# An encoder layer on one core: a longer last and first step at the two block boundaries, operand places on one grid, modulation pieces summed one per step, both transposes of a block in one go

## The chip, the cores and the metric

The kernel runs on one core of a Trainium2 chip. The metric is device time in microseconds of one launch. What is compared is the median of several executions; the profile is one execution, recorded in full.

## The reference

One layer of a bidirectional encoder over 256 positions of width 2048, float32, batch 1. Nine modulation vectors (a shift, a scale and a gate for each of three blocks) come from one product of silu(c) with a 2048 x 18432 matrix.

```python
mod = silu(c) @ w_ada + b_ada                   # sh1, sc1, g1, sh2, sc2, g2, sh3, sc3, g3
h = rms_norm(x, ffn1_pre_g) * (1 + sc1) + sh1   # modulate
x = x + 0.5 * g1 * rms_norm((silu(h @ w_gate) * (h @ w_up)) @ w_down, ffn1_post_g)
h = rms_norm(x, mix_pre_g) * (1 + sc2) + sh2
q, k, v, c_val, c_gate = split(h @ w_in)        # 8 heads of 128; conv branch of 1024
merged = concat([rms_norm(attention), rms_norm(conv branch)]) @ w_out
x = x + g2 * rms_norm(merged, mix_post_g)
h = rms_norm(x, ffn2_pre_g) * (1 + sc3) + sh3
x = x + 0.5 * g3 * rms_norm((silu(h @ w_gate) * (h @ w_up)) @ w_down, ffn2_post_g)   # D_FF = 5632
```

## The kernel before

The 256 positions are two halves t of 128 rows. Every weight matrix is read from HBM once, in chunks of 256 rows x 512 columns (512 KB, `wchunk`, L280): a load from SP's queue into one of 7 `raw` buffers, a rounding copy `hi` on ScalarE (L290), and the rest `lo` = raw - hi on VectorE (L291), in 4 buffer pairs. The activations are kept as hi and lo too. For each 128-row slice k of a chunk, and each half t, TensorE makes three products of 512 columns (L316 to L318: hi with xh, lo with xh, hi with xl), the weights moving and the activations stationary; a chunk is 12 products. `in_step` (L320) loads the chunks it is given, then multiplies all of them for t = 0 and after that all for t = 1, and ticks. A tick starts work put off by `defer` and lets each lane (a generator) advance by its rate.

`group` (L329) takes a whole product chunk by chunk; with `tail=4` the last four chunks are one step, so half 0 is done ahead of half 1, and with `head=4` the first four are.

A block boundary is `next_norm` (L409). The last group's half t is evicted (`ffn_down` L459, or L880), squared and summed (`post_block`), the four sums give a factor by way of GpSimd's pow (`post_rstd`), x is updated in four pieces and squared again (`post_add`, L405), a second pow gives the next norm's factor, and `pre_norm` (L360) scales x (`xn`, L368), transposes it on TensorE (L371), applies scale and shift on ScalarE (`hf`, L376) and splits it (L357, L358). There are two such boundaries: FFN1 to the mixer, whose first group `c0` is 8 chunks of w_in, and the mixer to FFN2, whose `begin2` takes the first gate and up group of stage 0 (two chunks each) as one step.

The modulation vectors are not products of TensorE: `mod_sum` (L169) loads 512 KB pieces of w_ada through the same `raw` buffers and adds them on VectorE, `acc = piece * c + acc` (L191), for a scale and a shift in turn; TensorE and ScalarE then sum over partitions (L206, L211). This runs as a lane beside the products. FFN1 is entered in four stages of K (`STAGES1`), FFN2 in three (`STAGES2`), so that products start while later slices of the modulation are still being summed; pieces are 512 columns wide (two sums a piece) or, for the last third of a FFN2 stage, 256 wide (four sums a piece).

`slot` (L249) hands out the shared places of a work pool by tag (`hh0`.., `ah0`.., `fs0`.., `gs`, `ac`). A place is 4096 bytes a partition, the two with tags `ah5` and `al5` are SLOT = 1144 elements, 4576 bytes. The places lie one after the other in order of first use, `al5` right behind `ah5`. `al5` holds the low part of the sixth block of `aT`.

In FFN's up products, `act_out` (L423) puts off the transposes of a finished block by `defer(AD, ..)` and `defer(AD + 1, ..)`: four transposes each, two chunks apart from the block's end and three. `rope_T` does the same for q and k.

## Time and profile before

| | us |
|---|---|
| median of 3 runs (lowest to highest) | 1952.46 (1952.25 to 1954.24) |
| the profiled execution | 1953.91 |
| its span | 1952.1 |
| TensorE busy | 1872.6 |
| VectorE busy | 1474.1 |
| ScalarE busy | 928.3 |

The span runs from the first instruction to the last; the profiled execution's own time is 1.8 us above it and 1.45 us above the median. Busy time of TensorE is an upper bound, since overlapping products count as busy to their modelled ends. Its granted clock is 1.00 (2.4 GHz) or 0.5 (1.2 GHz); a value between is a mean over a stretch.

### The profile page before, as it was taken

To read this page: it belongs to the slowest core of one execution; us is meant where nothing else is said; L and a number is where in the kernel's file an instruction comes from. 1 tells how busy PE (TensorE), PEld (TensorE's weight loads), DVE (VectorE), ACT (ScalarE), POOL (GpSimd) and SP (SyncE) were. 2 spreads that over 40 slices of the span, in tenths; PEclk is the share of its full clock that TensorE was granted. 3 is DMA by queue.
4 is the path that set the end of the run, shared out by engine and by line. 5 is a ranking of instruction groups with operands and counts; after the bars stand their busy time and mean duration, and the time that the engine had idled before them with its cause. 6 is when DMAs were issued, how large, how long until landed. Compare 5 with 4: busy or idle time off the path is not lost.

```text
span 1952.1 us, 23783 instructions
## 1 busy us (share of the span) xinstructions
PE 1872.6 (96%) x8358; PEld 1527.1 (78%) x8358; DVE 1474.1 (76%) x1824; ACT 928.3 (48%) x1428; POOL 66.0 (3%) x99
## 2 busy tenths in 40 slices
PE   2999999999999999899999988999999999999997
PEld 1888877888888888688888776687888888888886
DVE  6789999787777776689997777897786556545455
ACT  3554355444444444644456655534444443444442
POOL 2000000000000000000100000000000000000000
PEclk9999999999999999899999999999999999999999
DMA  9989978999999898357555767897777777666653
GB/s 344 310 297 311 323 253 283 348 340 328 314 321 316 317 318 292 109 184 224 173 165 161 239 214 258 301 341 254 226 247 244 244 253 248 195 185 191 206 191 101
DMA packets 250392, 496.29 MB, mean 254 GB/s; under 512 B 17209, under 2 KB 42625, under 8 KB 250272
## 3 DMA queue, kind: packets, MB, share of 16 engines
q1 hardware_dynamic: 247888, 491.38, 76.1%
q0 software_dynamic: 2208, 3.32, 0.5%
q8 instruction: 65, 1.06, 0.2%
q14 instruction: 55, 0.45, 0.1%
q10 hardware_dynamic: 176, 0.07, 0.0%
HBM read 492.58 MB, written 2.12 MB: 253 GB/s over the span
## 4 chain that ended last, share of the span: by engine, by line
PE 88%; DVE 5%; DMA 3%; ACT 2%; issue 2%; POOL 0%; DVEq 0%; POOLq 0%; ACTq 0%; SPq 0%
PE pd_t L318 8%; PE pd_t L317 8%; PE pd_t L316 8%; PE pg_t L317 8%; PE pg_t L318 8%; PE pg_t L316 8%; PE pu_t L318 8%; PE pu_t L317 8%; PE pu_t L316 7%; PE pc_t L316 2%; PE pc_t L318 2%; PE pc_t L317 2%; DVE acc L191 2%; DMA ada<-in_w_ada 1%; PE pa L384 1%
## 5 line engine op out<-in xcount | busy, mean ns | idle before, releaser
L191 DVE SCALAR_TENSOR_TENSOR acc<-ada,cact,acc 128x512 f32<-128x512 f32 (+2 forms) x448 | 384.9, 897 | 12.8 <-DMA acc<-in_b_ada 8.4
L291 DVE TENSOR_TENSOR lo_d<-raw_d,hi_d 128x1024 fp32r<-128x1024 f32 x176 | 215.3, 1225 | 157.6 <-ACT hi_d L290 156.9
L290 ACT CAST hi_d<-raw_d 128x1024 fp32r<-128x1024 f32 x176 | 185.2, 1052 | 261.2 <-PE pd_t L318 181.5
L290 ACT CAST hi_g<-raw_g 128x1024 fp32r<-128x1024 f32 x176 | 185.0, 1052 | 247.2 <-PE pg_t L318 121.0
L291 DVE TENSOR_TENSOR lo_g<-raw_g,hi_g 128x1024 fp32r<-128x1024 f32 x176 | 214.4, 1222 | 105.0 <-ACT hi_g L290 104.8
L291 DVE TENSOR_TENSOR lo_u<-raw_u,hi_u 128x1024 fp32r<-128x1024 f32 x176 | 213.9, 1222 | 104.7 <-ACT hi_u L290 104.4
L290 ACT CAST hi_u<-raw_u 128x1024 fp32r<-128x1024 f32 x176 | 184.8, 1052 | 214.0 <-PE pu_t L318 94.5
L318 PE MATMUL pd_t<-hi_d,a_0l 128*128 128x512 f32 x384 | 151.2, 394 | 0.0
L317 PE MATMUL pd_t<-lo_d,a_0h 128*128 128x512 f32 x384 | 150.5, 392 | 0.0
L316 PE MATMUL pd_t<-hi_d,a_0h 128*128 128x512 f32 x384 | 150.4, 392 | 0.0
L316 PE MATMUL pg_t<-hi_g,h3h 128*128 128x512 f32 x352 | 140.4, 401 | 5.3 <-ACT hi_g L290 4.2
L316 PE MATMUL pu_t<-hi_u,h3h 128*128 128x512 f32 x352 | 139.8, 400 | 2.9 <-ACT hi_u L290 2.9
L317 PE MATMUL pu_t<-lo_u,h3h 128*128 128x512 f32 x352 | 140.0, 398 | 1.7 <-DVE lo_u L291 1.6
L317 PE MATMUL pg_t<-lo_g,h3h 128*128 128x512 f32 x352 | 139.4, 396 | 1.7 <-DVE lo_g L291 1.7
L316 PE MATMUL pg_t<-hi_g,h1h 128*128 128x512 f32 x352 | 139.4, 398 | 1.0 <-ACT hi_g L290 1.0
L318 PE MATMUL pu_t<-hi_u,h3l 128*128 128x512 f32 x352 | 139.7, 397 | 0.0
L317 PE MATMUL pg_t<-lo_g,h1h 128*128 128x512 f32 x352 | 138.7, 394 | 0.8 <-DVE lo_g L291 0.8
L318 PE MATMUL pg_t<-hi_g,h3l 128*128 128x512 f32 x352 | 139.3, 396 | 0.0
L316 PE MATMUL pu_t<-hi_u,h1h 128*128 128x512 f32 x352 | 138.8, 396 | 0.0
L318 PE MATMUL pu_t<-hi_u,h1l 128*128 128x512 f32 x352 | 138.6, 394 | 0.0
L318 PE MATMUL pg_t<-hi_g,h1l 128*128 128x512 f32 x352 | 138.6, 395 | 0.0
L317 PE MATMUL pu_t<-lo_u,h1h 128*128 128x512 f32 x352 | 137.8, 392 | 0.1
(259 smaller groups left out, 3572.1 us busy)
## 6 DMA issues: line engine op xcount, KB each, us to landing
ada<-in_w_ada SPq DMA_DIRECT2D x288, 512.0 KB, 5.3
raw_g<-in_ffn_w_gate SPq DMA_DIRECT2D x176, 512.0 KB, 4.7
raw_u<-in_ffn_w_up SPq DMA_DIRECT2D x176, 512.0 KB, 4.7
raw_d<-in_ffn_w_down SPq DMA_DIRECT2D x176, 512.0 KB, 5.7
raw_c<-in_w_in SPq DMA_DIRECT2D x64, 256.0 KB, 3.1
raw_q<-in_w_in SPq DMA_DIRECT2D x16, 512.0 KB, 4.4
raw_k<-in_w_in SPq DMA_DIRECT2D x16, 512.0 KB, 4.5
raw_v<-in_w_in SPq DMA_DIRECT2D x16, 512.0 KB, 4.2
```

Source lines behind the costliest of these rows:

```text
L191: tc.keep_in_program_order(nc.vector.scalar_tensor_tensor(acc, w[:, j, :], cact[:, j0 + j:j0 + j + 1], acc, op0=ALU.mult, op1=ALU.add))
L290: nc.scalar.copy(h, r)
L291: nc.vector.tensor_tensor(l, r, f32(h), op=ALU.subtract)
L316: nc.tensor.matmul(o, xh, h, start=self.first and k == 0, stop=False)
L317: nc.tensor.matmul(o, xh, l, start=False, stop=False)
L318: nc.tensor.matmul(o, xl, h, start=False, stop=self.last and k == self.nk - 1)
L384: nc.tensor.transpose(ps[:, jj * S + t * P:jj * S + (t + 1) * P], src[:, t, jj * P:(jj + 1) * P], ident)
```

## The change

`mod_sum` loads and sums one piece and then yields, where it loaded a scale's and a shift's piece and summed both in turn. `group` loses `head`; the last step of FFN's last group is 7 chunks (`TAIL1`), and the last step of the mixer is both of the last two output blocks, 8 chunks. Three and four chunks of these steps get `hi`/`lo` in places of the work pool (`TAIL_AT1`, `TAIL_AT2`). The next block's first chunks are loaded before `next_norm`, four of them into such places (`HEAD_AT1`, `HEAD_AT2`); its first step is all 8 chunks of `c0`, or three groups of FFN2's stage 0 (6 chunks). Eviction of half t moves into `next_norm`. The SLOT size becomes a multiple of 64 elements, and a 64-byte tile `gap` is put ahead of the `h` places. The two deferred transposes of a block become one.

```diff
@@ -35,10 +35,14 @@
-HEAD = 4
-TAIL = 4
 JF = 4
+TAIL1 = 7
+TAIL_AT1 = (("hh2", "hl2"), ("hh3", "hl3"), ("gs", "ac"))
+HEAD1 = 8
+HEAD_AT1 = (("ah0", "al0"), ("ah1", "al1"), ("ah2", "al2"), ("ah3", "al3"))
+HEAD_AT2 = TAIL_AT2 = (("ah0", "ah1"), ("ah2", "ah3"), ("al2", "al3"), ("ah5", "al5"))
 CRATE = 1.8
...
@@ -51,7 +55,7 @@
 RAW = 7
 HILO = 4
-SLOT = 4 * (S + 2 * PAD)
+SLOT = -(-4 * (S + 2 * PAD) // 64) * 64
 STAGES1 = ((0, 4), (4, 8), (8, 12), (12, 16))
 STAGES2 = ((0, 4), (4, 10), (10, 16))
...
@@ -178,20 +182,16 @@
             accs.append(acc)
         kt = CH * BLK // n
         for j0 in range(0, NK, kt):
-            ws = []
-            for v in vs:
+            for v, acc in zip(vs, accs):
                 n0 = v * D + c0
                 raw = wpool.tile([P, CH, BLK], F32, tag="raw", bufs=RAW, name=f"ada{v}_{c0}_{j0}")
                 w = raw.rearrange("p a b -> p (a b)").rearrange("p (j n) -> p j n", n=n)
                 nc.sync.dma_start(w, w_ada[j0 * P:(j0 + kt) * P, n0:n0 + n].rearrange(
                     "(j p) n -> p j n", p=P))
-                ws.append(w)
-            for j in range(kt):
-                for w, acc in zip(ws, accs):
+                for j in range(kt):
                     tc.keep_in_program_order(nc.vector.scalar_tensor_tensor(
                         acc, w[:, j, :], cact[:, j0 + j:j0 + j + 1], acc,
                         op0=ALU.mult, op1=ALU.add))
-            for v in vs:
                 yield
         return accs
...
@@ -277,11 +277,16 @@
             return self.lo[k // 4][:, k % 4:k % 4 + n, :]
-    def wchunk(w, r0, kt, cols, name):
+    def wchunk(w, r0, kt, cols, name, at=None):
         raw = wpool.tile([P, CH, BLK], F32, tag="raw", bufs=RAW, name=f"raw_{name}")
-        hi = wpool.tile([P, CH, BLK], F32R, tag="hi", name=f"hi_{name}")
-        lo = wpool.tile([P, CH, BLK], F32R, tag="lo", name=f"lo_{name}")
+        if at is None:
+            hi = wpool.tile([P, CH, BLK], F32R, tag="hi", name=f"hi_{name}")
+            lo = wpool.tile([P, CH, BLK], F32R, tag="lo", name=f"lo_{name}")
+        else:
+            hi = slot(at[0], [P, CH, BLK], f"hi_{name}", F32R)
+            lo = slot(at[1], [P, CH, BLK], f"lo_{name}", F32R)
         r, h, l = raw[:, :kt, :], hi[:, :kt, :], lo[:, :kt, :]
         n = BLK // len(cols)
         for m, n0 in enumerate(cols):
...
@@ -317,22 +322,26 @@
                 nc.tensor.matmul(o, xh, l, start=False, stop=False)
                 nc.tensor.matmul(o, xl, h, start=False, stop=self.last and k == self.nk - 1)
-    def in_step(work):
-        hls = [g.load(c) for g, c in work]
+    def load_all(work, places=()):
+        return [g.load(c, places[n] if n < len(places) else None) for n, (g, c) in enumerate(work)]
+    def in_step(work, places=(), hls=None):
+        if hls is None:
+            hls = load_all(work, places)
         for t in range(NT):
             for (g, c), hl in zip(work, hls):
                 g.products(c, t, hl)
         for _ in work:
             tick()
-    def group(*args, head=0, tail=0, **kw):
+    def group(*args, tail=0, places=(), **kw):
         g = Group(*args, **kw)
-        head = min(head, g.chunks - tail)
-        mid = range(head, g.chunks - tail)
-        for cs in (range(head), *([c] for c in mid), range(g.chunks - tail, g.chunks)):
-            in_step([(g, c) for c in cs])
+        for c in range(g.chunks - tail):
+            in_step([(g, c)])
+        if tail:
+            in_step([(g, c) for c in range(g.chunks - tail, g.chunks)], places)
     def square_sum(src, dst, name):
...
@@ -406,18 +415,17 @@
             square_sum(xs, sx[:, db:db + 1], "jx")
         return rstd_parts(sx, D, f"r{i}_{t}", keep_in="rx")
-    def next_norm(f, ssp, A, B, j1, i):
-        hT = Parts(f"h{i}", "h", range(4))
-        jh = min(HEAD * CH, j1)
+    def next_norm(hT, f, ssp, A, B, j1, i, evict):
+        evict(0)
         rs = [post_add(f, post_rstd(ssp, i, 0), i, 0)]
         pre_norm(hT, rs, A, B, 0, JF, i, 0, 1)
+        evict(1)
         rs.append(post_add(f, post_rstd(ssp, i, 1), i, 1))
-        pre_norm(hT, rs, A, B, JF, jh, i, 0, 1)
-        pre_norm(hT, rs, A, B, 0, jh, i, 1, 2)
-        pre_norm(hT, rs, A, B, jh, j1, i)
-        return hT, rs
+        pre_norm(hT, rs, A, B, JF, j1, i, 0, 1)
+        pre_norm(hT, rs, A, B, 0, j1, i, 1, 2)
+        return rs
     def act_out(aT, i, gs, pu, name):
...
@@ -430,9 +438,12 @@
             src = transposed(ac[:, :, q * 256:(q + 1) * 256], tr_ps(f"pa{name}_{q}"))
             split_to(aT, k0 + 2 * q, 2, src)
+        def turns():
+            turn(0)
+            turn(1)
         aT.add(i)
-        defer(AD, lambda: turn(0))
-        defer(AD + 1, lambda: turn(1))
+        defer(AD, turns)
     def gs_tile(name):
         return work.tile([P, NT, BLK], F32, tag="gs", name=f"gs{name}")
...
@@ -451,14 +462,19 @@
         for db in range(4):
             pd = mm_ps(f"pd{i}_{th}_{db}")
             group(pd, aT, wd, ba * 4, (bb - ba) * 4, db * BLK, f"d{i}_{th}_{db}",
-                  tail=TAIL if th == 1 and db == 3 else 0)
-            for t in range(NT):
+                  tail=TAIL1 if th == 1 and db == 3 else 0, places=TAIL_AT1)
+            def evict(t, db=db, pd=pd):
                 if th == 0:
                     nc.scalar.copy(f[db][:, t, :], pd[t])
                 else:
                     nc.vector.tensor_tensor(f[db][:, t, :], pd[t], f[db][:, t, :], op=ALU.add)
-                if th == 1:
                     post_block(f, ssp, G, t, db)
+            if th == 1 and db == 3:
+                return evict
+            for t in range(NT):
+                evict(t)
     ROUNDS = ((0, 6, (0, 1, 2, 3, 4, 5)), (6, 11, (0, 1, 2, 3, 5)))
...
@@ -562,17 +578,15 @@
     rs = [rstd_parts(sx[t], D, f"r0_{t}", act=True, keep_in="rx") for t in range(NT)]
     for _ in first:
         pass
+    nc.vector.memset(work.tile([P, 16], F32, name="gap"), 0.0)
     hT = Parts("h1", "h", range(4))
     pre_norm(hT, rs, A1, B1, *STAGES1[0], "1_0")
     def begin2(open_group, run, order):
-        gs, k1 = {}, STAGES2[0][1]
-        for w, b in order[:2]:
-            ps = mm_ps(f"p{w}2_{b}_0")
-            gs[w, b] = open_group(w, b, 0, 0, k1, ps)
-        in_step([(g, c) for g in gs.values() for c in range(g.chunks)])
-        return {k: (g.ps, k1) for k, g in gs.items()}, k1
+        in_step(ahead2, hls=hls2 + load_all(ahead2[4:]))
+        return {k: (g.ps, STAGES2[0][1]) for k, g in heads2.items()}, len(ahead2)
     load_cols(("conv_b", "conv_ln_g", "conv_ln_b", "attn_out_g", "conv_out_g"), 1)
     g1, g2, g3 = [keep.tile([P, NK], F32, name=f"gc{i}") for i in (1, 2, 3)]
...
@@ -586,10 +600,17 @@
     aT = ffn_start(hT, a["ffn1_w_gate"], a["ffn1_w_up"], 1, STAGES1, ffn1_mods,
                    lambda s: pre_norm(hT, rs, A1, B1, *STAGES1[s], f"1_{s}"),
                    (later_mods(), LRATE))
-    f, ssp = ffn_rest(hT, aT, a["ffn1_w_gate"], a["ffn1_w_up"], a["ffn1_w_down"],
-                      lambda: gate_tile(g1, 1), 1)
+    f, ssp, evict = ffn_rest(hT, aT, a["ffn1_w_gate"], a["ffn1_w_up"], a["ffn1_w_down"],
+                             lambda: gate_tile(g1, 1), 1)
     drain_all()
-    hT, rs = next_norm(f, ssp, A2, B2, NK, 2)
+    QC = BLK // 2
+    hT = Parts("h2", "h", range(4))
+    ps_c0 = mm_ps("pc0")
+    c0 = Group(ps_c0, hT, a["w_in"], 0, NK, (3 * AW, 3 * AW + CW), "c0")
+    ahead = [(c0, c) for c in range(HEAD1)]
+    hls = load_all(ahead[:4], HEAD_AT1)
+    rs = next_norm(hT, f, ssp, A2, B2, NK, 2, evict)
+    in_step(ahead, hls=hls + load_all(ahead[4:]))
     w_in = a["w_in"]
...
@@ -654,8 +675,11 @@
             pst = transposed(ra[:, :, q * 256:(q + 1) * 256], tr_ps(f"prt_{name}_{q}"))
             nc.scalar.copy(T[:, 2 * q:2 * q + 2, :], pst)
-        defer(RD, lambda: turn(0))
-        defer(RD + 1, lambda: turn(1))
+        def turns():
+            turn(0)
+            turn(1)
+        defer(RD, turns)
         return T
     scale = HD ** -0.5
...
@@ -873,22 +896,46 @@
     drain(conv_entry)
     drain(mods)
     r2 = rc["conv"]
-    for db in range(4):
-        po = mm_ps(f"pc{db}")
-        group(po, mT, w_out, 8, 8, db * BLK, f"oc{db}", kx=8, tail=TAIL if db == 3 else 0)
-        for t in range(NT):
-            nc.vector.scalar_tensor_tensor(f[db][:, t, :], po[t], r2[:, t:t + 1],
-                                           f[db][:, t, :], op0=ALU.mult, op1=ALU.add)
-            post_block(f, ssp, G2, t, db)
-    hT, rs = next_norm(f, ssp, A3, B3, STAGES2[0][1], 3)
+    pcs = [None] * 4
+    def conv_group(db):
+        pcs[db] = mm_ps(f"pc{db}")
+        return Group(pcs[db], mT, w_out, 8, 8, db * BLK, f"oc{db}", kx=8)
+    def evict_c(db, t):
+        nc.vector.scalar_tensor_tensor(f[db][:, t, :], pcs[db][t], r2[:, t:t + 1],
+                                       f[db][:, t, :], op0=ALU.mult, op1=ALU.add)
+        post_block(f, ssp, G2, t, db)
+    for db in range(2):
+        g = conv_group(db)
+        for c in range(g.chunks):
+            in_step([(g, c)])
+        for t in range(NT):
+            evict_c(db, t)
+    both = [conv_group(db) for db in (2, 3)]
+    in_step([(g, c) for g in both for c in range(g.chunks)], TAIL_AT2)
+    def evict(t):
+        for db in (2, 3):
+            evict_c(db, t)
+    hT = Parts("h3", "h", range(4))
+    heads2 = {}
+    for w, b in (("g", 0), ("u", 0), ("g", 1)):
+        heads2[w, b] = Group(mm_ps(f"p{w}2_{b}_0"), hT, a["ffn2_w_gate" if w == "g" else "ffn2_w_up"], 0,
+                             STAGES2[0][1], b * BLK, f"{w}2_{b}_0_0")
+    ahead2 = [(g, c) for g in heads2.values() for c in range(g.chunks)]
+    hls2 = load_all(ahead2[:4], HEAD_AT2)
+    rs = next_norm(hT, f, ssp, A3, B3, STAGES2[0][1], 3, evict)
     aT = ffn_start(hT, a["ffn2_w_gate"], a["ffn2_w_up"], 2, STAGES2, ffn2_mods,
                    lambda s: pre_norm(hT, rs, A3, B3, *STAGES2[s], f"3_{s}"),
                    (mod_gate(8, "ffn2_post_g", 0.5, g3), 0.3), begin2)
-    f, ssp = ffn_rest(hT, aT, a["ffn2_w_gate"], a["ffn2_w_up"], a["ffn2_w_down"],
-                      lambda: gate_tile(g3, 3), 2)
+    f, ssp, evict = ffn_rest(hT, aT, a["ffn2_w_gate"], a["ffn2_w_up"], a["ffn2_w_down"],
+                             lambda: gate_tile(g3, 3), 2)
     for t in range(NT):
+        evict(t)
         r = post_rstd(ssp, 4, t)
         for db in range(4):
             s = slice(db * BLK, (db + 1) * BLK)
...
```

## Rows read from the trace of the kernel before

**Rows 1.** The page's first part: busy us (share of the span) xinstructions.
```profile
PE 1872.6 (96%) x8358; PEld 1527.1 (78%) x8358; DVE 1474.1 (76%) x1824; ACT 928.3 (48%) x1428; POOL 66.0 (3%) x99
```
**Rows 2.** Stretches: length, busy time (count) of each engine, TensorE's granted clock, DMA share, GB/s.
```profile
112.20:290.00 177.80, 177.56 (x802) 145.16 (x801) 169.33 (x216) 84.04 (x122) 2.88 (x4) 1.00 0.89 297
...
799.30:815.40 16.10, 7.64 (x22) 5.46 (x22) 12.10 (x27) 11.43 (x31) 2.17 (x7) 0.58 0.40 127
...
1166.40:1180.70 14.30, 5.69 (x16) 4.21 (x16) 11.04 (x23) 9.44 (x25) 1.59 (x3) 0.64 0.45 143
1187.00:1256.00 69.00, 62.57 (x257) 48.05 (x256) 58.76 (x89) 35.44 (x67) 3.88 (x6) 0.95 0.93 323
...
1337.00:1350.00 13.00, 9.30 (x29) 7.07 (x29) 9.29 (x19) 3.14 (x3) 0.00 (x0) 0.74 0.90 304
```
**Rows 3.** Timeline at the first boundary: start us, length us, engine, line, operation [idle before <-releaser].
```profile
793.98 0.69 DVE L459 TENSOR_TENSOR f<-pd_t,f 128x512 f32<-128x512 f32 x1 [3.23 <-PE pd_t L318]
798.17 1.05 ACT L290 CAST hi_c<-raw_c 128x1024 fp32r<-128x1024 f32 x1 [0.34 <-PE pd_t L318]
798.17 2.08 DVE L405 SCALAR_TENSOR_TENSOR x<-f,pr,x 128x512 f32<-128x512 f32 x3 [0.46 <-POOL pr L352]
...
802.46 0.63 ACT L339 ACTIVATE jx<-x 128x512 f32<-128x512 f32 x1
803.17 2.35 DVE L291 TENSOR_TENSOR lo_c<-raw_c,hi_c 128x1024 fp32r<-128x1024 f32 x2
805.44 0.15 DVE L350 TENSOR_REDUCE s_r<-sx 128x1 f32<-128x4 f32 x1
806.43 0.63 DVE L368 TENSOR_SCALAR xn<-x,r 128x256 f32<-128x256 f32 x2 [0.59 <-POOL r L352]
806.84 1.12 PE L371 MATMUL pst<-ident,xn 128*128 128x128 f32 x4 [7.35 <-DVE xn L368]
809.07 0.79 PE L316 MATMUL pc_t<-hi_c,h2h 128*128 128x512 f32 x1 [1.12 <-ACT h2h L357]
```
**Rows 4.** Timeline at the second boundary, the same columns.
```profile
1161.08 0.75 DVE L880 SCALAR_TENSOR_TENSOR fm<-pc_t,rcc,fm 128x512 f32<-128x512 f32 x1 [1.99 <-PE pc_t L318]
1174.03 1.12 PE L371 MATMUL pst<-ident,xn 128*128 128x128 f32 x4 [7.50 <-DVE xn L368]
1180.63 0.88 DVE L368 TENSOR_SCALAR xn<-x,r 128x256 f32<-128x256 f32 x3 [0.66 <-POOL r L352]
1182.30 0.60 PE L371 MATMUL pst<-ident,xn 128*128 128x128 f32 x4
1182.72 1.16 ACT L376 ACTIVATE hf<-pst,B,A 128x128 f32<-128x128 f32 x3 [0.56 <-PE pst L371]
1184.87 0.58 ACT L507 COPY sumu<-pu_t 128x512 f32<-128x512 f32 x1
```
**Rows 5.** Timeline of TensorE: products of the last group of FFN1's second round.
```profile
786.41 0.39 PE L317 MATMUL pd_t<-lo_d,a_1h 128*128 128x512 f32 x1
789.16 0.39 PE L317 MATMUL pd_t<-lo_d,a_1h 128*128 128x512 f32 x1
791.45 0.40 PE L318 MATMUL pd_t<-hi_d,a_1l 128*128 128x512 f32 x1
793.78 0.40 PE L316 MATMUL pd_t<-hi_d,a_1h 128*128 128x512 f32 x1
```
**Rows 6.** Timeline of VectorE: runs of modulation sums (L191), the same columns.
```profile
25.59 10.02 DVE L191 SCALAR_TENSOR_TENSOR acc<-ada,cact,acc 128x512 f32<-128x512 f32 x15
392.85 2.60 DVE L191 SCALAR_TENSOR_TENSOR acc<-ada,cact,acc 128x1024 f32<-128x1024 f32 x2
698.10 3.67 DVE L191 SCALAR_TENSOR_TENSOR acc<-ada,cact,acc 128x1024 f32<-128x1024 f32 x3
1230.88 3.25 DVE L191 SCALAR_TENSOR_TENSOR acc<-ada,cact,acc 128x256 f32<-128x256 f32 x8
1332.21 6.42 DVE L191 SCALAR_TENSOR_TENSOR acc<-ada,cact,acc 128x256 f32<-128x256 f32 x16
```

More of the change, by code (lines that the diff above doesn't have):

```diff
@@ L302, in __init__, with load @@
             self.chunks = -(-nk // CH)
-        def load(self, c):
+        def load(self, c, at=None):
             kt = min(CH, self.nk - c * CH)
-            return wchunk(self.w, (self.k0 + c * CH) * P, kt, self.cols, f"{self.name}_{c}")
+            return wchunk(self.w, (self.k0 + c * CH) * P, kt, self.cols, f"{self.name}_{c}", at)
         def products(self, c, t, hl):
@@ L528, in ffn_rest @@
             G = gate() if th == 1 else None
-            ffn_down(f, aT, wd, ba, bb, th, G, ssp, i)
-        return f, ssp
+            evict = ffn_down(f, aT, wd, ba, bb, th, G, ssp, i)
+        return f, ssp, evict
     A1, B1 = affine_tiles(1)
@@ L616, in encoder_layer, with in_group @@
         nc.gpsimd.memset(u[:, :, PAD + S:], 0.0)
-    def in_group(o, name, head=0):
+    def in_group(o, name):
         ps = mm_ps(f"p{name}")
-        group(ps, hT, w_in, 0, NK, o, name, head=head)
+        group(ps, hT, w_in, 0, NK, o, name)
         return ps
@@ L830, in encoder_layer @@
     rc = {}
-    QC = BLK // 2
     conv_entry = None
     for g in range(CW // QC):
-        ps = in_group((3 * AW + g * QC, 3 * AW + CW + g * QC), f"c{g}", head=HEAD if g == 0 else 0)
+        ps = in_group((3 * AW + g * QC, 3 * AW + CW + g * QC), f"c{g}") if g else ps_c0
         gs = gs_tile(f"c{g}")
```

## The prediction, made before the changed kernel was run

> **What bounds the kernel now.** I read the first part of the page, then the stretches stage by stage, then the timeline where TensorE stops. TensorE is busy 96% of the span, VectorE 76%, ScalarE 48% [rows 1]. So time can only come from stretches where TensorE waits or runs at the lower clock, or from the pace of its products. Three of the four that lie near the change are at block boundaries or right behind one [rows 2]. A product at full clock is 0.229 us (12 between two rows 2.75 us apart) [rows 5], a transpose 0.15 at most (four in 0.60) [rows 4].
>
> At the first boundary, 16.1 us hold 22 operations: 14 products and 8 transposes, worth 4.4 us; 11.7 us are lost. At the second, 14.3 us hold 12 products and 4 transposes, worth 3.4; 10.9 are lost. In both the clock's mean is about 0.6: it fell to 1.2 GHz after the idle time. FFN2's stage 0 (69 us) loses 6.4 us idle and 3.5 to the clock (mean 0.95): 9.9. The end of stage 1 (13 us) loses 3.7 and 3.4: 7.1. Together 40 us. The other places: the start, and what follows the last product.
>
> **First boundary.** Half 0 is done 24 products (5.5 us) ahead of half 1. Its chain runs from the eviction at 793.98 to the scaled x at 806.43, 12.45 us; TensorE idles 7.35 us, and the first product of the next block comes 2.64 us after that, at 809.07 [rows 3]. With 7 chunks in the last step the lead is 42 products, 9.6 us. What the chain needs undisturbed: 4.2 us to the first update of x; four updates at 0.68, 2.7; the last square, 0.63 and its readout, 0.9; the sum, pow and scaling (805.44 to 806.43), 1.0: 8.8. The difference, 3.6, is in the rows: half 1's eviction and squares, weight copies of 1.05 us on ScalarE, and a pair of `lo` of 2.35 us on VectorE ahead of the last sum [rows 3]. Moving half 1's eviction behind removes a part. The four `hi` in places are new on the chain's engines: the second to fourth wait until half 1 has passed chunks 1, 3 and 5 of the step, 1.4, 4.1 and 6.9 us behind half 0's end, and behind them in ScalarE's order stand the squares, behind their `lo` the updates. So 8.8 to 12.45; I take 10, nearer the undisturbed sum since three of four copies fall before the squares. First product: 10 + 2.64 + 0.15 (start of the eviction) - 9.6 = 3.2 us behind the last one, against 9.7 now: 6.5 gained (3.9 to 7.7). Of the 11.7 lost, 9.1 are this wait (9.7 less four transposes) and 2.6 the slow clock; a wait of 3 us may still bring it (one of 3.7 did at 1337 [rows 2]): 0 to 2.6, I take half. The new first step is 96 products and 32 transposes, 22 to 26.8 us; ScalarE has in it 16 times two slices of a half at 1.08 (two of them from 1182.72 to 1184.87) [rows 4], five squares at 0.8 and four copies at 1.05: 25.5. No slack, so 1 us back (0 to 2). Net -7 (-2 to -10.5). The loads come before `next_norm` on SP and go ahead of the constants and of the conv weights, whose place is now held by a weight chunk; their wait would hold up SP, but 16 loads stand before it and half 1 is past that chunk by then: nothing.
>
> **Second boundary.** The chain starts at 1161.08, its transposes at 1174.03, after 7.5 us of idle time [rows 4]; the first product is 2.2 us behind them as at the first (806.84 to 809.07) [rows 3]. The lead grows from 24 to 48 products, 11.0 us. To the transposes it was 12.95, undisturbed 8.8 and 0.4 as above. Two blocks are now evicted per half, one more update and square, 0.9: 10.1 to 13.85; I take 11.5. First product 11.5 + 2.2 - 11.0 = 2.7 us behind the last one, against 9.9 now: 7.2 gained (4.8 to 8.6). New wait: half 1's factor is there at 1180.63, 14.3 us behind the last product [rows 4]. The new step's half 0 is 36 products, so it ends 11.4 us behind; with the second block, half 1 comes at 12 to 16. Now late: 0.6 to 5 us; I take 2. Clock: 0 to 1.7 back, 0.5. Net -5.5 (0 to -9.5). The third group's PSUM needs the evictions of half 0, which are earlier.
>
> **Modulation sums.** A sum on the accumulator that the sum before it wrote starts later than one on another. Two on one accumulator take 2.60 us; three on two accumulators in turn 3.67 [rows 6]. One sum lasts x, so the starts are 2.60 - x apart on one accumulator and (3.67 - x) / 2 on two: with x = 1.28, the length of one in this trace, 1.32 and 1.19. That is 0.12 us. Before, scale and shift alternate; after, a 512 piece has one such pair, a 256 piece three. There are 112 of the first (16 in each of seven stages) and 16 of the second (8 in two): 160 pairs, 19 us of VectorE. In FFN1's stages VectorE is busy 169.3 of 177.8 us [rows 2]; 1.9 us a stage fit in, barely: +1 (0 to +3). At the start 15 sums end the wait [rows 6]: seven pairs, +0.9, but the scale's half is done two sums earlier, -0.7 to +1, I take +0.5. The Trainium skill, VectorE: DVE Perf Modes (The DRAIN you can't avoid), says that instructions chained on VectorE take the same time with and without a semaphore between them. By that both terms would be nothing and the time 1.5 us lower; the 1.32 against 1.19 disagrees.
>
> The gain is in the bursts. In stage 1 sixteen sums of two pairs of 256 pieces run as one block of 6.42 us [rows 6]; `lo` waits behind, and TensorE idles 3.7 of the 13 us from 1337 on [rows 2]. One piece is 4 sums, 2.0 us (0.40 each and three pairs). I take -4.5 (0 to -7): a wait of VectorE for the transposed sums remains. In stage 0 the blocks are 3.25 us [rows 6]. There the work itself is the limit: 18 chunks of products remain behind the new first step, 49.5 us; VectorE has in that time 14 to 18 `lo` at 1.18 (two in 2.35) [rows 3], 32 sums at 0.67 (15 in 10.02) and 32 at 0.40 [rows 6], 34.2, and 4.8 for 40 of the pairs: 55.5 to 60 us. With four chunks in places, two `lo` and some pieces can go ahead during the first step, an estimated 7 us. So 0 to 5 us of waits by the work, some clock, against 9.9 now: -3.5 (+3 to -8).
>
> **Places.** `al5` starts behind a place of 4576 bytes, 32 off a multiple of 64. In the products of that block the pace is 0.233 (10 in 2.33 us from 791.45), before them 0.229 [rows 5]. 4 slices, 4 output blocks, 2 halves, 3 products, 2 rounds, 2 FFNs: 384 products, -1.5 us (0 to -1.5). The Trainium skill, SBUF — State Buffer (Specifications (TRN2)), gives lines of 16 bytes; by it a start at 32 is as good as one at 64 and the edit is worth nothing. The rows disagree. `gap` itself is one fill of 16 elements. It moves the activations' places by 64 bytes, onto the remainder by 128 that the weights' buffers have; no product before has both so, and none shows a price. I take 0 and make it a rival.
>
> **The rest.** One interruption of eight transposes for two of four saves a few ns each, 26 times: 0; they need both transposing banks at once, +1 at most. The end: half 1's chain is unchanged, 0.
>
> **Sum.** -7 - 5.5 + 1 + 0.5 - 4.5 - 3.5 - 1.5 = -20.5. From the profiled execution's 1953.9 that is 1933.4; it stood 1.45 above the median, so **1932**. The bounds together are -37 and +6, which don't fall together; this case is 1922 to 1943.
>
> **Rivals.** *VectorE becomes the bound in the modulated stages.* For: 95% busy in FFN1, and the sum above for stage 0. Against: four chunks of lead in `hi` and `lo`. Then stage 0 costs 2 more, stage 1 keeps its 7.1, FFN1 and the start cost 3 and 1: -7 - 5.5 + 2 - 1.5 + 4 = -8, 1944.5 (1940 to 1952). *The lead stays empty:* the copies into places stand in the chain's way, the first boundary gains 2 and the second nothing: 1942.5; with the first rival 1953. For: all four waits are new. Against: 3.6 us of disturbance already are in the 12.45. *Slower: the pace.* If with all operands on one remainder the products run at 0.233 as those of `al5` do, 7680 products less 384 cost 0.0042 each, 30.5 us, and the 1.5 isn't gained: 1964. It decides from two thirds of the products on. For: the pace is seen to hang on where an operand starts. Against: a shift by 64 leaves both at the start of a 64-byte step, unlike `al5`. The other way round, a better pace, has no row at all.
>
> **Chances.** Forecast 0.64, VectorE 0.17, empty lead 0.07, pace 0.10, still better 0.02. The range 1921 to 1948 leaves out the slow pace, a part of the first two rivals together, and what lies below. 0.2% is 3.9 us, about what a measurement can tell from no change: faster 0.81 (forecast, better, and most of the first two rivals), same 0.08, slower 0.11.
>
> **What would show it.** Right: TensorE's idle time ahead of the boundary transposes falls from 7.4 and 7.5 to 2 us or less, and the mean clock there rises; no block of 256 sums over 2.2 us in stage 1, and no stop of TensorE there; the products of `al5` at 0.229. Wrong: runs of products at 0.233 outside; stops of TensorE behind `lo` in FFN1's stages; ScalarE full in the first step of the mixer with TensorE waiting for `h2h`.

## The result and the profile after

The kernel after takes **1926.01 us** (median of 4 runs, 1924.82 to 1926.93), the kernel before 1952.54 on the same chip: ratio **0.9862**, 95% interval 0.9845 to 0.9879. Faster, by 26.5 us; the prediction had 1932 and 20.5. The profiled execution took 1925.6, its span is 1923.8.

The page's first part, and the stretches that answer to [rows 2] (most of FFN1's stages 1 to 3, first boundary, second boundary, FFN2's stage 0):

```profile
PE 1849.4 (96%) x8358; PEld 1522.2 (79%) x8358; DVE 1478.2 (77%) x1829; ACT 929.2 (48%) x1440; POOL 68.5 (4%) x99
```

```profile
113.10:288.30 175.20, 174.71 (x796) 143.93 (x795) 168.51 (x215) 82.97 (x121) 2.88 (x4) 1.00 0.90 299
790.90:806.00 15.10, 9.93 (x38) 7.05 (x36) 13.26 (x32) 12.24 (x32) 3.05 (x7) 0.77 0.62 193
1158.90:1172.50 13.60, 7.80 (x25) 5.74 (x24) 13.09 (x24) 9.01 (x23) 2.17 (x2) 0.75 0.58 171
1176.00:1245.00 69.00, 63.41 (x281) 49.59 (x280) 56.92 (x91) 38.64 (x76) 3.88 (x6) 1.00 0.85 291
```

The count of instructions on TensorE is what it was [rows 1], its busy time 23 us less. At the boundaries the clock's mean rose from about 0.6 to 0.76, and FFN2's stage 0 holds 281 operations in 69 us where it held 257. The pace, in the products that answer to [rows 5]; those from 788.35 on read the block of `al5`:

```profile
786.31 0.39 PE L321 MATMUL pd_t<-hi_d,a_1h 128*128 128x512 f32 x1
...
788.35 0.39 PE L321 MATMUL pd_t<-hi_d,a_1h 128*128 128x512 f32 x1
...
790.39 0.39 PE L321 MATMUL pd_t<-hi_d,a_1h 128*128 128x512 f32 x1
```

Nine products in 2.04 us, twice: 0.2267 each, in the block of `al5` too. Before it was 0.229 in most of the trace and 0.233 in that block [rows 5]. Taken by triples of products (hi, lo, hi) that the next triple follows without a stop, 2187 of 2297 last 680 ns now; before, 2006 of 2251 lasted 686 or 687 and 190 lasted 700, nearly all of these in the blocks of `al5` and in FFN1's stage 0. The first boundary, as in [rows 3]:

```profile
781.75 0.69 DVE L471 TENSOR_TENSOR f<-pd_t,f 128x512 f32<-128x512 f32 x1 [7.21 <-PE pd_t L323]
...
785.60 1.06 ACT L295 CAST hi_c<-raw_c 128x1024 fp32r<-128x1024 f32 x1 [1.40 <-PE pd_t L322]
786.79 0.63 ACT L348 ACTIVATE jx<-x 128x512 f32<-128x512 f32 x1
787.42 1.03 ACT L295 CAST hi_c<-raw_c 128x1024 fp32r<-128x1024 f32 x1
...
788.98 1.05 ACT L295 CAST hi_c<-raw_c 128x1024 fp32r<-128x1024 f32 x1
789.74 2.35 DVE L296 TENSOR_TENSOR lo_c<-raw_c,hi_c 128x1024 fp32r<-128x1024 f32 x2
790.55 1.04 ACT L295 CAST hi_c<-raw_c 128x1024 fp32r<-128x1024 f32 x1
792.61 0.14 DVE L359 TENSOR_REDUCE s_r<-sx 128x1 f32<-128x4 f32 x1
792.67 1.21 DVE L296 TENSOR_TENSOR lo_c<-raw_c,hi_c 128x1024 fp32r<-128x1024 f32 x1
793.81 0.14 DVE L360 TENSOR_SCALAR s_r<-s_r 128x1 f32<-128x1 f32 x1
793.87 1.21 DVE L296 TENSOR_TENSOR lo_c<-raw_c,hi_c 128x1024 fp32r<-128x1024 f32 x1
794.03 1.46 POOL L361 TENSOR_TENSOR r<-s_r,mhalf 128x1 f32<-128x1 f32 x1 [2.50 <-DVE s_r L360]
795.52 0.62 DVE L377 TENSOR_SCALAR xn<-x,r 128x256 f32<-128x256 f32 x2 [0.44 <-POOL r L361]
795.93 1.11 PE L380 MATMUL pst<-ident,xn 128*128 128x128 f32 x4 [4.70 <-DVE xn L377]
798.16 0.79 PE L321 MATMUL pc_t<-hi_c,h2h 128*128 128x512 f32 x1
```

The chain of half 0 now lasts 13.77 us (781.75 to 795.52) where it lasted 12.45. Three `hi` copies stand between its squares, and a `lo` between the sum of the squares and the step that follows it. The pow on GpSimd (L361) then runs beside another `lo` and lasts 1.46 us; in the kernel before it ran beside none and lasted 0.54. TensorE idles 4.70 us instead of 7.35. The second boundary, as in [rows 4], shows the same: a chain of 15.1 us, 4.69 idle.

```profile
1148.43 0.75 DVE L906 SCALAR_TENSOR_TENSOR fm<-pc_t,rcc,fm 128x512 f32<-128x512 f32 x1 [3.15 <-PE pc_t L323]
...
1163.55 0.62 DVE L377 TENSOR_SCALAR xn<-x,r 128x256 f32<-128x256 f32 x2 [0.44 <-POOL r L361]
...
1163.96 1.11 PE L380 MATMUL pst<-ident,xn 128*128 128x128 f32 x4 [4.69 <-DVE xn L377]
```

And the waits of TensorE in the later part of the mixer (990 to 1165; waited for, total, times, longest). The first is the second boundary's, 7.50 before; of the others only the 1.3 for the attention's factor stood there before, with nothing else over 0.3:

```profile
PE pst L380 <- DVE xn L377: 4.7, 1, 4.7
PE ptc L798 <- ACT repc L794: 2.4, 1, 2.4
PE pse L715 <- ACT Tq L676: 1.8, 1, 1.8
PE psrl L823 <- POOL ra L361: 1.3, 1, 1.3
```

**Where the 28.3 us between the two spans went**, worked out from the starts of the products, stage by stage: 7680 products at 2.2 ns less, 17.1, and about 2.5 for those that ran at 0.233; first boundary 5.6, second 2.3; FFN2's stage 0 4.4 and stage 1 6.4; given back, 0.6 at the start and 9.3 in the mixer between the boundaries. The 9.3 is counted against a better pace of all the mixer's products, about 2.8 there. With the better pace alone (the first run below) the products from c1 to the end of `w_out` gain 1.0 of it. So 1.8 of the 9.3 is pace that does not turn into time there, and 7.5 to 8 is what the other edits cost. More than half of the whole is the pace, for which the prediction had 1.5.

### The profile page after: what moved, and what is told of

The parts are those of the page before. It is cut to its first block, busy times and chain, and to the rows that moved or that the text cites. A ratio compares the mean times of both kernels' runs of the same rounds, so it can differ in the third digit from the quotient of the medians.

```text
span 1923.8 us, 23711 instructions
## 1 busy us (share of the span) xinstructions
PE 1849.4 (96%) x8358; PEld 1522.2 (79%) x8358; DVE 1478.2 (77%) x1829; ACT 929.2 (48%) x1440; POOL 68.5 (4%) x99
## 4 chain that ended last, share of the span: by engine, by line
PE 86%; DVE 7%; DMA 2%; ACT 2%; issue 2%; POOL 0%; SPq 0%; DVEq 0%; POOLq 0%; ACTq 0%
PE pd_t L323 8%; PE pd_t L322 8%; PE pd_t L321 8%; PE pg_t L321 8%; PE pg_t L322 8%; PE pg_t L323 8%; PE pu_t L322 7%; PE pu_t L323 7%; PE pu_t L321 7%; DVE acc L192 3%; PE pc_t L321 2%; PE pc_t L323 2%; PE pc_t L322 2%; DMA x<-in_x 1%; PE pa L393 1%
## 5 line engine op out<-in xcount | busy, mean ns | idle before, releaser
L192 DVE SCALAR_TENSOR_TENSOR acc<-ada,cact,acc 128x512 f32<-128x512 f32 (+2 forms) x448 | 397.2, 899 | 11.8 <-DMA acc<-in_b_ada 7.8
```

Source lines behind the costliest of these rows:

```text
L192: tc.keep_in_program_order(nc.vector.scalar_tensor_tensor(acc, w[:, j, :], cact[:, j0 + j:j0 + j + 1], acc, op0=ALU.mult, op1=ALU.add))
```

## The experiments

All medians against runs of the kernel before on the same chip (1951.8 to 1953.1).

**The places alone.** The kernel before with two lines of the change:

```diff
-SLOT = 4 * (S + 2 * PAD)
+SLOT = -(-4 * (S + 2 * PAD) // 64) * 64
...
+    nc.vector.memset(work.tile([P, 16], F32, name="gap"), 0.0)
```

> The kernel before with the two edits of the operand places alone (the size of a place rounded up to 64 bytes, and the fill called gap that moves the activations' places by 64 bytes); work, order and waits stay those of the kernel before. Theory A (the pace of the products made most of the change): a triple of products took 686.7 ns before and takes 680.0 after, 2.2 ns a product, times 7680 is 17.1 us, and the products that ran at 233.3 ns (those of al5 and those of FFN1's stage 0) give 3 more: about 1933 us, 228.9 ns a product becoming 226.7. Rival B (the pace came with the other edits, by the order of work or less contention, and the places are worth al5's 1.5 us alone, as in the prediction): 1951 us, pace 228.9.

1937.43 us, ratio 0.9927 (0.9913 to 0.9942): -14.8. 2080 of 2252 triples last 680 ns. Theory A holds, B falls. (The first line makes a place 4608 bytes, a multiple of 256 and not only of 64.) It is somewhat less than 20, since where TensorE isn't the only limit the pace is not the time: the mixer's `w_in` went from 216.6 to 216.2 us only.

**The gap taken out of the kernel after.** The line with `gap` goes, all else stays.

> The kernel after without the fill called gap, so that the activations' places start 64 bytes lower, on the remainder by 128 that they had before; all else as after. Theory A (pace by where the operands start): products back at 228.9 ns, 1926 + 17 = 1943 us. Rival B (the gap is worth nothing): 1926 us and 226.7 ns.

1938.63 us, 0.9935 (0.9918 to 0.9951): 12.6 slower than the kernel after, and nearly all triples back at 686 to 687. One fill of 16 elements is worth about half of the whole change. Where the weights of a long step lie in activation places, both operands at one remainder, triples of 680 appear in this kernel too: it is the pair that counts, not the 64 bytes. The pace does not change at once there. At 786.99, where half 1 enters such places, the triples last 698, 691, 697 and 684 ns and then 680.

**The operands' starts, measured alone.**

> A kernel that computes nothing of the reference: 26 blocks of 24 triples of products in the kernel's own pattern (hi with xh, lo with xh, hi with xl; 128 x 512 moving, 128 x 128 stationary, one accumulator for a block), the start of the moving operand and that of the stationary one each set to a number of bytes behind a multiple of 128. The block's tile is q and two letters, first the moving operand's start, then the stationary one's: a is 0, b 16, c 32, d 48, e 64, f 80, g 96, h 112, i 128. Six more blocks (b and two letters) run while ScalarE and VectorE copy and subtract 128 x 1024 tiles. Theory A1 (what counts is the distance of the two starts by 128): 0.2267 us a product for qaa, qee, qcc, qgg, qia and qai, 0.229 for qea and qae (64 apart), 0.2333 for qac, qag, qce, qeg and the other pairs 32 apart; 72 products then take 16.3, 16.5 and 16.8 us. Theory A2 (what counts is that both lie 64 behind, or that the stationary one does): 0.2267 for qee and qae alone, qaa at 0.229. Rival B (it is the order of work and the traffic of the other engines, not the places): all q blocks alike, and the b blocks slower than the q blocks of the same letters.

Each figure is a mean over a block's products. At equal starts (aa, cc, ee, gg) 0.2267; 64 apart with the moving one ahead (ea, gc) 0.2289; 64 apart the other way (ae, cg) 0.2333; 32 apart, either way, 0.2333; 128 apart (ia, ai) 0.2324. With ScalarE and VectorE at work: aa 0.2267, ea 0.2290, ee 0.2267, eg 0.2333, the same as without. B falls, A2 too; A1 was wrong on 128 and on the sign of the distance. At 16 bytes it is not one rule: ba 0.2317, ab 0.2267, bb 0.2300.

**Farther apart, each pair twice.**

> A kernel that computes nothing of the reference: again blocks of 24 triples of products, the start of the moving and that of the stationary operand each at a multiple of 64 bytes behind the same remainder by 512 (letters a to i: 0, 64, 128 ... 512; the tile is q or r, then the moving operand's letter, then the stationary one's). Each pair runs twice, q in one order and r in the reverse. Theory A1' (both starts at the same remainder by 256 or 512 give 0.2267 us, all else is slower): qaa, qbb and qcc 0.2267, qia and qai too, qca and qac (128 apart) 0.2324 as in the run before, qba 0.229 and qab 0.2333; the r blocks like the q blocks. Theory A3 (a block keeps a phase that it falls into at its start, and the start of the operands only makes one more likely): the q and r blocks of the same pair differ, as FFN1's first stage ran at 0.2333 in one trace and at 0.229 in another at the same places.

A1' holds for these blocks. What counts is the moving start less the stationary one, by 256. From the rows, 60 products each (first and last start): difference 64, 13.73 us; 128, 13.93; 192, 14.00; 256, 13.60.

```profile
60.97 0.39 PE L89 MATMUL qba<-mov,sta 128*128 128x512 f32 x1
74.70 0.39 PE L89 MATMUL qba<-mov,sta 128*128 128x512 f32 x1
...
77.48 0.39 PE L89 MATMUL qca<-mov,sta 128*128 128x512 f32 x1
91.41 0.40 PE L89 MATMUL qca<-mov,sta 128*128 128x512 f32 x1
...
94.21 0.39 PE L89 MATMUL qda<-mov,sta 128*128 128x512 f32 x1
108.21 0.39 PE L89 MATMUL qda<-mov,sta 128*128 128x512 f32 x1
...
110.98 0.39 PE L89 MATMUL qea<-mov,sta 128*128 128x512 f32 x1
124.58 0.39 PE L89 MATMUL qea<-mov,sta 128*128 128x512 f32 x1
```

All 23 pairs fall into these four classes, in both orders (one block of 46 at 0.2333 where its repetition had 0.2324). In the kernel before, weights start 64 ahead of the activations: 0.2289, as measured; `al5` is 96 off: 0.2333. In the kernel after the difference is 0. Two things in the kernel go beyond these pairs. Only the third product of a triple reads `al5`, yet in the kernel before its triples last 700 ns as a whole, each of the three products longer than elsewhere; no block here mixes two differences. And one stage had two paces at the same starts (see Open).

**The sums alone.** The kernel before with the new loop of the sums:

```diff
-            for j in range(kt):
-                for w, acc in zip(ws, accs):
...
+            for v, acc in zip(vs, accs):
...
+                for j in range(kt):
```

> The kernel before with the new order of the modulation sums alone (one piece in each step, both accumulators no longer in turn). By the prediction: start +0.5, FFN1's stages +1, stage 1 of FFN2 -4.5, stage 0 -3.5: -6.5, 1946 us. By the two traces compared, where the same stages lost 0.6 more at the start, about the same in FFN1, 4.4 less in stage 0 and 6.4 less in stage 1: -10, 1942 us. Rival (stage 0's gain comes from the new first step's chunks in places and not from the sums): 1947 us, with stage 0 as before.

1950.12 us, 0.9990 (0.9981 to 1.0000): -2.1, with an interval from -3.7 to 0. FFN2's stage 1 gained 7.0 (109.2 to 102.2), the start lost 0.5, FFN1's stages 1 to 3 moved by 0.2 in all, stage 0 lost 0.5: there the rival holds. Unforeseen: the first products of `w_out` lost 5.3 (87.7 to 93.0), 1.6 of it at half clock, the rest in two waits in this trace:

```profile
PE ptc L770 <- ACT repc L766: 2.2, 1, 2.2
PE psc L202 <- DVE acc L188: 1.8, 1, 1.8
```

**The boundaries alone.** The kernel before with the longer lead, the copies into places and half 1's eviction behind half 0's chain.

> The kernel before with the new boundaries alone (7 and 8 chunks of lead, copies into places, half 1's eviction behind half 0's chain); sums, places' size and interruptions as before. By the prediction -7 and -5.5: 1940 us. By the two traces compared -5.6 and -2.3: 1944.5 us, if the mixer's middle stays as before. Rival (the 9 us that the middle of the mixer lost beside a better pace come with the boundaries, since the first step of the mixer leaves its conv work and its sums later): 1952 us, no gain at all.

1942.07 us, 0.9948 (0.9934 to 0.9963): -10.2. First boundary -5.9, second -1.8, FFN2's stages 0 and 1 -2.1 and -3.4; +1.8 in the first 100 products behind the mixer's first step, and +2.4 in `w_out`. TensorE waits for the chain 4.6 us:

```profile
PE pst L384 <- DVE xn L381: 4.6, 1, 4.6
```

Neither this nor the sums alone bring stage 0 its 4.4: it takes both. The kernel without the gap has both, at the old pace, and gains 4.6 there. The three parts add up: -14.8 - 2.1 - 10.2 = -27.1. That they do is in part luck, since stage by stage they don't: in FFN2's stage 1 the three gain 2.2, 7.0 and 3.4 by themselves and 7.4 together, since in part the same waits go; over the whole of `w_out` they change the time by -0.6, +5.3 and +2.4, and by +3.5 together.

**The transposes in two interruptions again.**

```diff
-        defer(AD, turns)
+        defer(AD, lambda: turn(0))
+        defer(AD + 1, lambda: turn(1))
```

The same with `RD`.

> The kernel after with the transposes of a block again in two interruptions, one step apart (for the FFN's activations and for the rotated q and k). The middle of the mixer lost time in the kernel after: TensorE waits 2.17 us once ahead of the transposes of the attention weights, for ScalarE's copy of the rotated block out of the second transposing bank. Theory M (two banks taken in one step make that wait): the stop goes, the stretch of w_in behind the mixer's first step goes from 220.0 us to about 218, and the whole to 1924. Rival (the stop is made by the longer lead, or by the sums, which shift when that copy comes): the stop stays, 1926.

1925.10 us, 0.9866 (0.9850 to 0.9882), not to be told from the kernel after. Theory M holds for the stop and not for the total: `w_in` falls from 220.0 to 218.1 us, but the two traces end alike. Time comes back in `w_out`, where TensorE waits 1.4 us instead of 0.5 for a sum (`psc`), and in FFN2, whose own transposes are split here too and which takes 2.0 longer up to the second round's down products. The wait of 1.8 becomes

```profile
PE pse L717 <- DVE sm L702: 0.2, 1, 0.2
```

**Sums sooner in the mixer.** The rotated blocks' transposes split, and `MRATE` from 0.8 to 1.2.

> The kernel after with the rotated blocks' transposes in two interruptions, and with the rate of the modulation sums beside the first products of w_out raised from 0.8 to 1.2 pieces a chunk. In the kernel after 4 pieces of sums are left at the end of that stretch, behind VectorE's work for the convolution's factor, and hold 4 of the 7 raw buffers that the next weights need: ScalarE's copies wait for the weights' transfers, the copy of the factor stands behind these copies, and TensorE waits 2.79 us for it. If so the stop falls to about 0.6 us as in the kernel before, and with the other stop of 2.17 gone the time is 1926 - 2.2 - 2 = 1922 us. Rival (the sums only move to where VectorE is as full, and the time comes back as waits for lo earlier in that stretch): 1924 to 1926.

1923.27 us, 0.9853 (0.9839 to 0.9868). The time lies between the two forecasts. The wait for the factor's copy is gone, but two others are in its place, so 1.3 of its 2.4 were gained in that stretch and the rival is half right:

```profile
PE psc L206 <- issue: 1.7, 1, 1.7
...
PE po_t L322 <- DVE lo_oa L296: 1.0, 2, 0.7
```

**The chain first.** Copies of chunks 3 to 7 (3 to 5 at the second boundary) kept in program order behind half 0's chain and first block:

```diff
-    hls = load_all(ahead[:4], HEAD_AT1)
+    hls = load_all(ahead[:3], HEAD_AT1)
...
+    rs = next_norm(hT, f, ssp, A2, B2, NK, 2, evict, lambda: hls.extend(
+        load_all(ahead[3:], HEAD_AT1[3:], pin=tc.keep_in_program_order)))
...
         pre_norm(hT, rs, A, B, 0, JF, i, 0, 1)
+        mid()
         evict(1)
```

> The kernel after with five of the first step's copies (chunks 3 to 7, at both boundaries) put behind the chain of half 0 and its first transposed block on ScalarE and VectorE, where they now stand between its squares and its updates. In the kernel after the first boundary's chain runs from 781.75 to 795.52, 13.8 us where the prediction had 10; five copies of 1.04 us on ScalarE and four of 1.2 on VectorE lie in it. Theory C (the copies lengthen the chain): its length falls to about 10 us and TensorE's idle time ahead of the first transposes from 4.7 to about 1. What it does to the time: if the copies were merely in the wrong order, 2 to 3 us a boundary, 1921 us; if ScalarE's work over the whole boundary is the limit (25.5 us in a step of 22 to 27, by the prediction), the copies are then waited for one step later, and the time stays at 1926 or rises.

1932.18 us, 0.9896 (0.9879 to 0.9912): 6 slower. The first boundary, its timeline and then TensorE's waits:

```profile
781.97 0.69 DVE L472 TENSOR_TENSOR f<-pd_t,f 128x512 f32<-128x512 f32 x1 [7.21 <-PE pd_t L323]
...
791.32 0.54 POOL L361 TENSOR_TENSOR r<-s_r,mhalf 128x1 f32<-128x1 f32 x1 [5.19 <-DVE s_r L360]
...
791.90 0.97 DVE L377 TENSOR_SCALAR xn<-x,r 128x256 f32<-128x256 f32 x3 [0.66 <-POOL r L361]
792.41 0.69 PE L380 MATMUL pst<-ident,xn 128*128 128x128 f32 x4 [0.96 <-DVE xn L377]
...
795.49 4.84 ACT L295 CAST hi_c<-raw_c 128x1024 fp32r<-128x1024 f32 x5
```

```profile
PE pst L380 <- ACT hf L385: 3.2, 1, 3.2
PE pc_t L323 <- DVE h2l L367: 2.7, 1, 2.7
```

The chain falls to 9.93 us and the idle time ahead of the transposes to 0.96: the copies did lengthen it by 3.8. Of this 0.9 came by way of GpSimd, whose pow lasts 0.54 us again. At the second boundary the chain falls to 11.3 us. But the copies have to be made somewhere, and now TensorE stops behind them inside the step.

**First stages' sums in turn.** Transposes of the rotated blocks split, and in `stage_mods` the pieces from `k0 == 0` on in the old order:

```diff
-            yield from mod_affine(vsh, vsc, gname, A, B, k0 * P, n * P)
+            yield from mod_affine(vsh, vsc, gname, A, B, k0 * P, n * P, k0 == 0)
```

> The kernel after with two edits that the runs so far point to: the rotated blocks' transposes again in two interruptions, and the sums of each FFN's first stage (at the start, and beside the first products of w_out) again with both accumulators in turn, two pieces a step; all other sums one piece a step. By the runs so far: the stretch of w_out that took 87.3 to 87.7 us with the sums in turn takes 90.1 to 93.0 with one piece a step, so -3 to -4; the wait of 2.2 us for the second transposing bank goes, -1.9; the start gives back up to 0.6. 1926 - 5 = 1921 us. Rival (the 3 us come back, since the sums that end late in the mixer were only part of what TensorE waits for there): 1924 us, as without the edit of the sums.

**1921.91 us**, 0.9848 (0.9835 to 0.9861). The median is 4.1 less than that of the kernel after, 2.7 by the ratios, whose intervals overlap. `w_out` went from 91.4 to 88.1, `w_in` from 220.0 to 218.2; 1.5 of the first is a stretch at half clock that is missing here, as it is with the split transposes alone (see Open); so the sums in turn bring 1.8 of the 3.3, or 2.8 against the run with the split alone. The wait for the factor's copy fell to

```profile
PE ptc L802 <- ACT repc L798: 1.0, 1, 1.0
```

**The copies spread.** The version of 1921.91 with one copy behind each two blocks of half 0 (a block is one `xn` of 256 columns). All of these blocks now come ahead of half 1's eviction, so half 1's chain moves too, and not the copies alone.

> The version of the run before (rotated blocks' transposes in two interruptions, the first stages' sums in turn) with the first step's copies of chunks 3 to 7 spread: one behind each two transposed blocks of half 0, instead of five in a row behind the first as in the run with the chain first. There the chain fell from 13.8 to 9.9 us and TensorE's idle time ahead of the first transposes to 1, but five copies of 4.84 us stood between the first blocks and the next, TensorE stopped 3.2 and 2.7 us behind them, and the time rose by 6 us. Theory (only the order was wrong, there is room between the blocks): the stops inside the step go, each boundary gains 2 to 3 us, 1917 us. Rival (ScalarE's and VectorE's work over the boundary is the limit, in whatever order): the idle time ahead falls to 1 us, as much is lost inside the step, 1922 to 1925 us.

1919.67 us, 0.9833 (0.9819 to 0.9847); its interval overlaps the last version's, and the time lies between the two forecasts. The profiled spans are both 1918.6, but the profiled execution was the fastest of that version and the slowest of this one. At the first boundary TensorE's gap ahead of the first product is 4.0 shorter and the step behind it 4.0 longer:

```profile
PE pc_t L329 <- DVE lo_c L303: 2.0, 2, 1.3
PE pst L396 <- DVE xn L393: 1.6, 2, 1.0
PE pc_t L328 <- ACT hi_c L302: 0.5, 1, 0.5
```

At the second boundary it is 4.1 and 4.1. So at the boundaries the rival holds: nothing of the 2 to 3 us is gained at either, two orders of the same copies give the same end and a third a worse one. That the work as such is the limit is argued and not shown: from 791 to 826 ScalarE is busy 29.7 of 35 us and VectorE 24.5. The median is 2.2 below the last version's, by the ratios not told apart from it; against the kernel after the two intervals barely touch.

## Why the prediction was right in the total and wrong in its parts

- **Total.** 1926.0 lies in the forecast's range, and that is luck: the sum that led there was made of other parts. Without the gap, which the prediction put at nothing, the change brings 13.6 (1938.63), where the sum had 20.5; the gap's 12.6 fill the hole.
- **Places, -1.5, and `gap`, 0.** The term that was mis-sized. Alone the two edits give -14.8, the gap 12.6 of the change. The step that failed is "no product before has both so, and none shows a price; I take 0". The rows showed that the pace hangs on where an operand starts, and the one rival made of it pointed the wrong way: that products at one remainder would run at 0.233. They run at 0.2267. The other way round was given 0.02 for want of a row; lack of a row is no reason against a sign. By the 16-byte lines (the Trainium skill, SBUF — State Buffer, Specifications (TRN2)) alone a shift by 64 would change nothing, as the prediction read them; 0.2267 against 0.2289 shows that it does.
- **First boundary, -7.** -5.6. The chain was put at 10 us and took 13.8. Of the four copies in places three did fall before the squares of x, as the prediction said (the third at 785.60, the first square at 786.79). The step that failed is that the other "four copies at 1.05" were counted into the new step alone. In the kernel's text they stand behind `next_norm`, but nothing pins them there. They ran ahead: ScalarE had made all eight by 794.70, and their `lo` stood in the chain as well. With chunks 3 to 7 pinned behind, the chain took 9.93, the prediction's 10. Then 2.0 are given back behind the step (c1's first 100 products; 1.8 with the boundaries alone), where the prediction had 1 for want of slack on ScalarE. That reason is not what the trace shows: ScalarE is busy 21.5 of the step's 27.8 us, and TensorE waits for nothing in the step or in those products. Six of the eight transposes of the convolution's weights (L628), which came before c1 in the kernel before, stand between its first products now (825.97 to 829.45).
- **The pow.** The prediction took the sum, pow and scaling at 1.0 us; they took 2.9, 1.1 for a `lo` in between and 0.9 for the pow. It lasts 0.54 us alone and 1.44 to 1.65 us where a `lo` of VectorE has begun just before it, in the traces of the kernels before and after, of the chain first and of the copies spread; in each such case it ends 0.4 us behind the `lo`.
- **Second boundary, -5.5.** -2.3. The chain was put at 11.5 and took 15.1, for the same reason; with the copies pinned it took 11.3. Idle time fell to 4.7 at both, so the sign of being right, 2 us or less, did not come.
- **FFN1's sums, +1.** 0: the 1.9 us a stage fitted in.
- **Start, +0.5.** +0.6, and the pair's 0.12 holds: the 15 sums last 10.90 us where they lasted 10.02 [rows 6], seven pairs of 0.126. What the Trainium skill states (VectorE: DVE Perf Modes, The DRAIN you can't avoid), that a semaphore behind each instruction of a chain costs nothing extra, does not speak of a chain against independent instructions; the prediction's reading of it would have had 10.02.
- **Stage 1, -4.5.** -6.4, and -7.0 with the sums alone; the mechanism as told. One block of seven sums still lasts 2.86 us, where the sign asked for 2.2 at most, but TensorE does not stop for it. Its only wait there is

```profile
PE pst L380 <- DVE xn L377: 0.5, 1, 0.5
```

- **Stage 0, -3.5.** -4.4, but by sums and boundaries together; alone they gave +0.5 and -2.1.
- **Merged transposes, 0, "+1 at most".** The wait for the second bank costs 1.8 once, and undoing the merge moves the whole by less than can be told. In the FFN the merge gains a little: FFN2's stage 2 takes 102.2 us in the five traces that have it and the new pace, and 102.5 in the two with the new pace and the split.
- **The mixer was not in the sum.** It lost 9.3: about 2.0 behind its first step, 3.1 around the attention's transposes (1.8 of it the wait that goes when they are split; the rest is pace that `w_in` does not turn into time with the places alone either), 1.5 at half clock, 2.7 at the factor's copy. The sums' change was followed into the start and the modulated stages, but not into the one stage where sums run beside `w_out` and hold the raw buffers of the next weights.
- **VectorE as the bound** (0.17) did not come; nor the empty lead (0.07), though half of it did. The two together were put at 1953; the terms given add up to 1955.

**Open.** FFN1's stage 0 ran at 0.2333 in the traces of before and of the sums alone, and at 0.2289 with the boundaries alone and without the gap, at the same operand starts and clock. And the stop of 1.3 us ahead of the attention's factor, in every trace, is followed by 3.4 us at half clock in five (the kernel after, sums, boundaries, chain first, spread) and not in the others:

```profile
1074.00:1083.00 9.00, 7.24 (x35) 5.75 (x34) 6.34 (x15) 8.52 (x18) 1.80 (x3) 0.81 0.20 64
```

for the kernel after, and for the kernel before

```profile
1085.00:1094.00 9.00, 7.24 (x41) 5.82 (x40) 6.58 (x15) 8.90 (x20) 1.80 (x3) 1.00 0.24 77
```

## What to carry to other kernels

Where TensorE is busy 96% of the span, 1% of pace (19 us here) is worth more than any single stop: look at where its two operands start, and price a shift of operands by a small run with products alone, in both signs. A longer lead only helps if the work that fills it does not stand on the engines of the chain it is to cover; count that engine's work over the whole boundary before counting the lead. Work whose text stands behind a chain may run ahead of it unless it is pinned; pinning alone did not pay here. A change to a shared generator has to be followed into every stage that it runs in.

## What the runs showed of the hardware

The pace of blocks of 128 x 512 products with a weight load each depends on the moving operand's start less the stationary one's, by 256 bytes: 0.2267 us at 0, 0.2289 at 64, 0.2324 at 128, 0.2333 at 192 and 32 or 96 apart either way (0.2343 in one block). Four pairs with ScalarE and VectorE at work gave the same. Equal starts at 16 behind a multiple of 32 gave 0.2300, and one stage of the full kernel ran at 0.2333 in two traces and at 0.2289 in two at a difference of 64: cases left open.

A pow on GpSimd takes 0.54 us by itself and ends 0.4 us behind a VectorE subtraction of 128 x 1024 that began just before it (1.46 against 0.54 in the two chains shown).
